# Gates in the middle of the attention, output tiles at its last units, one small load on GpSimd's queue and two column sums in two rounded parts

## The chip, the cores and the metric

The kernel runs on one core of a Trainium2 chip. A time is that of one execution on the device, in microseconds (us), and the median of several runs is compared. The core has five engines with queues of their own, which meet only at semaphores: TensorE (PE, matrix products and transposes; PEld is its weight load), VectorE (DVE), ScalarE (ACT), GpSimd (POOL) and SyncE (SP, which here only issues transfers). GpSimd can issue transfers too. Each engine works through its queue strictly in order.

## The reference

One layer of an encoder for 512 positions of width 1024, in float32, with two groups of heads side by side:

```python
h = rmsnorm(x, norm_mix); proj = h @ w_in          # c_q 768 | c_kv 256 | k_pe 32 | u_h 3 x 512
q = (rmsnorm(c_q) @ w_uq)  ; kv = rmsnorm(c_kv) @ w_ukv      # 8 heads, 64 + 32 wide keys, 64 wide values
q, k = rope(rmsnorm(q)), rope(rmsnorm(k))
y_attn = softmax(q k^T / sqrt(96)) v
x0, x1, vh = split(dwconv3(u_h))
y_hyena = x0 * (long_conv(x1 * vh, filters) + bias)          # the "gate" is this product with x0
y_mix = concat(rmsnorm(y_attn), rmsnorm(y_hyena)); x = x + y_mix @ w_out
g, u = split(dwconv3(rmsnorm(x) @ w_up)); x = x + (silu(g) * u) @ w_down
x = x + sigmoid(x @ w_ple_gate) * rmsnorm(p @ w_ple)
```

The long convolution is computed by products with cosine and sine tables. Each rmsnorm needs, for every position, the sum of squares over the features; features lie on the partitions, so that sum is a product with a matrix of ones.

## The kernel before, in words

Data lies transposed, 128 features on the partitions and 512 positions along a row. To keep float32 accuracy with the faster float32r products, each operand is split into a rounded high part (written by ACT) and the remainder (written by DVE), and each product takes three matmuls: high times high, high times low, low times high. `wload` brings a 128x1024 block of weights through SP's queue (`wr`), rounds it on ACT (`wh`), and makes the remainder on DVE, or for half of some blocks by ACT and an adding transfer of GpSimd's queue (`wl`).

The program goes through these stages: the input projection (from the first matmul at 6.3 us to 147 us, with the filters and the forward transforms of the convolution between), the keys and queries and the inverse transforms (to 196 us), the attention (scores from 196.4 to 262.0 us, its last products to 271 us), the output projection, the wide up projection with its short convolutions (to about 554 us), the down projection (to 680 us), and the gate of the embedding with the stores.

The attention is 32 units, a unit being one head for 128 of the query positions. For unit n PE makes the scores (three matmuls into `ax`), DVE takes their row maximum (`TENSOR_REDUCE st`), ACT takes the exponential (`pr`), DVE or GpSimd divides by the sum, PE transposes `pr` with the identity, ACT and DVE split the transposed block (`pth`, `ptl`), and PE multiplies it with the values (eight matmuls of 256 columns per unit pair half). The loop that emits this (`for n in range(NU + LAG + 2)`, line 1381 of before) puts two other kinds of work between the units:

- `gate(c)`, line 1227, for the four feature blocks c: four transposes on PE, three products on DVE, and for the norm a square on ACT and an add. Behind it the gated block is split (ACT and DVE) into the operands `yh`. Block 0 is emitted ahead of the loop, the others at the units named in `GN`.
- `hyena_out(m)`, line 1322, for the eight output tiles: twelve matmuls of `w_out` with `yh`, a product with the norm's factor `Rh` on DVE, a load of the block of x and an add on GpSimd. Three of the tiles are emitted at the units named in `FILLS`, five behind the loop. `Rh` is made at unit `NRH`.

Behind the loop `rms_bcast(Ra, acc5, ...)` makes the factor of the attention's norm: the ones product, then Ln and Exp with one correction step on ACT and DVE, then the products and splits of `ys` into `ya`, which the second half of the output projection reads. Four of the hyena tiles (`RFILL`) stand on PE between the ones product and the first matmul that reads `ya`.

`rms_bcast` (line 612) is called for six factors. Its ones product is in plain float32; in the trace it is two matmul records.

The order of instructions is not the order of the code. A planner (`Plan`) records all operations, gives each a due time from PE's recorded order, and then lays them out engine by engine with a cost for each kind of operation, taking at each step the earliest due of those that could start. The constants at the head (`D_...`, the delays with which side tasks are started, `GN`, `FILLS`, `NRH`, the order `UQ` of the query tiles, `TAIL`, and the table `ENG`, which says which engine does a given operation) and the allowance `MARGIN` between engines set the result.

Of the kernel before, what the change touches and what calls it, by code (L numbers as in the profile page):

```python
# [19 lines left out]
P = 128  # L20
T = 512
# [2 lines left out]
T_UQ = 3.9  # L24
T_K = 1.3
D_SIN = 2.0
D_FILT = 13.0
D_TR = 2.0
D_HALF = 7.0
D_RMS = 30.5  # L30
D_LAT = 0.0
D_UU = 13.0
D_UT = 0.5
D_MUL = 3.0
D_SPR = 3.5
D_SQ = 2.0
NTMP = 10
D_LR = 12.0
D_KC = 6.0
D_RC = 4.0  # L40
W0N = 512
W0B = 2
W1A = 3
W1B = 4
KLAG = 2.0
NRH = 15
D_FT = 8.0
TAIL = 'R E0 E1 O P V0 S0 S1 V1 S2 G0 V2 S3 V3'
ENG = {'pr0': 'G', 'a53': 'V', 'a64': 'V', 'sp3': 'V', 'pr2': 'G', 'sp7': 'G', 'qa2': 'V', 'm5': 'V', 'a51': 'G', 'ah1': 'G', 'hl0': 'V', 'fwo': 'G', 'ah3': 'G', 'qa5': 'V', 'hl2': 'G', 'qa3': 'V', 'm6': 'V', 'm7': 'G', 'm2': 'V', 'qa1': 'V', 'sp5': 'G', 'xt': 'G', 'Uc': 'G', 'sp4': 'G', 'w01': 'V', 'w11': 'V', 'a61': 'G', 'pr3': 'G', 'a67': 'G', 'a63': 'V', 'u4': 'G', 'a65': 'G', 'w10': 'G', 'u3': 'G', 'sp0': 'G', 'eos': 'V', 'vx': 'V', 'vl': 'V', 'vh': 'A', 'va': 'A', 'vf': 'V', 've': 'A', 'vc': 'A', 'sx': 'A', 'sl': 'A', 'sh': 'A', 'sa': 'V', 'sf': 'V', 'se': 'A', 'sc': 'A', 'qa4': 'G', 'sp6': 'V', 'm4': 'V', 'rot2': 'G', 'cv5': 'V', 'm1': 'G', 'a62': 'V', 'rot1': 'G', 'ah0': 'V'}
ATT = {'pr', 'a', 'ah', 'hl', 'xt'}  # L50
PRI = {'rows': 500, 'val': 20, 'kt': 60, 'rms': -120, 'cols': 400, 'H': 0, 'gate': 150, 'uT': -120, 'io': -20, 'sq': 20, 'turn': 0, 'so': -300, 'fold': -120, 't8': 0, 'gsq': -50, 'ie': 400}
QACT = 0
UQ = [5, 0, 4, 1, 2, 3]
D_KS = 2.0
D_KR = 7.0
D_TAIL = 14.5
RFILL = 4
RPRI = 0
LAG = 3
NPR = 4  # L60
FILLS = (16, 24, 32)
GN = [4, 6, 5, 11]
CPRI = 50
EPS = 1e-6
MARGIN = 0.05
AIM = 0.0
STRETCH = {'V': 1.05, 'S': 1.03, 'G': 1.05, 'PE': 1.0, 'SP': 1.0}
NH = 8
# [390 lines left out]
def tile_encoder_block(  # L459
# [19 lines left out]
    const = plan.pool("const", 1)
# [13 lines left out]
    def atile(dt=F32R):  # L493
        return apool.tile([P, T], dt, tag="a", name="a")
# [88 lines left out]
    gm = const.tile([P, 8], F32, tag="gm", name="gm")  # L583
    par = const.tile([P, NPAR], F32, tag="par", name="par")

    def pcol(name, i=0, p0=0, p1=P):
        return par[p0:p1, POFF[name] + i : POFF[name] + i + 1]

    ident = const.tile([P, P], F32, tag="ident", name="ident")
    ones = const.tile([P, P], F32, tag="ones", name="ones")  # L590
    G.memset(ones, 1.0)

    eps = const.tile([P, 1], F32, tag="eps", name="eps")
# [17 lines left out]

    def rms_bcast(out, ssq, n, tmp, key):
        ps = ax_ps()
        PE.matmul(ps, ones, ssq, start=True, stop=True)
        with pri("rms"):
            rsqrt(out, tmp(), tmp(), ps, n, key)

# [26 lines left out]
    def tmp(dt=F32):  # L644
        return ft.tile([P, T], dt, tag="t", name="t", bufs=NTMP)
# [21 lines left out]
    for k in range(8):  # L667
        t = xpool.tile([P, T], F32, tag="x", name="x")
        SP.dma_start(t, xT[k // 2][:, (k % 2) * T : (k % 2 + 1) * T])
        xraw.append(t)  # L670
        if k == 0:
            SP.dma_start(gm, g_mix)
            first = load_part(0, w0, 0, W0N)
        for at_k, m, w, a, b in ((W0B, 0, w0, W0N, 1024), (W1A, 1, w1, 0, T), (W1B, 1, w1, T, 1024)):
            if k == at_k:
                halves.setdefault(k, []).append((f"w{m}{int(a > 0)}", *load_part(m, w, a, b)))
# [4 lines left out]
    for k in range(8):  # L681
        h, l = atile(), atile()
# [9 lines left out]
    x0 = [gp.tile([P, T], F32, tag=f"x0{c}", name=f"x0{c}") for c in range(4)]  # L692
# [528 lines left out]
    yh = []  # L1221
# [5 lines left out]
    def gate(c):  # L1227
        ps = mm_ps()
        for b in range(4):
            PE.transpose(ps[:, b * P : (b + 1) * P], yt[b][:, c * P : (c + 1) * P], ident)  # L1230
        pb = ps.rearrange("p (a b) -> p a b", a=4)
        with pri("gate"):
            V.tensor_tensor(even_blocks(x0[c]), even_blocks(x0[c]), pb[:, 0:2, :], op=ALU.mult)
            V.tensor_tensor(odd_up(x0[c]), odd_up(x0[c]), pb[:, 2, :], op=ALU.mult)
            V.tensor_tensor(odd_down(x0[c]), odd_down(x0[c]), pb[:, 3, :], op=ALU.mult)
        with pri("gsq"):
            if c == 0:
                S.activation(acch, x0[c], AF.Square)
# [4 lines left out]
        with pri("so"):
            h, l = atile(), atile()
            split(h, l, x0[c], pcol("g_oh", c))
            yh.append((h, l))
# [75 lines left out]
    def hyena_out(m):  # L1322
        ps = out_mm(m, 1, yh)
        xt = xpool.tile([P, T], F32, tag="x", name="x")
        SP.dma_start(xt, xT[m // 2][:, (m % 2) * T : (m % 2 + 1) * T])
        t = tmp1()
        V.tensor_tensor(t, ps, Rh, op=ALU.mult)
        e("xt", "G").tensor_tensor(xt, xt, t, op=ALU.add)
        xm.append(xt)

    def turn(n):
# [48 lines left out]
    for n in range(NU + LAG + 2):  # L1380
        if n < NU:
            if n % 4 == 0 and 1 < n // 4 + 1 < NH:
                prep(n // 4 + 1, ap_ if n // 4 % 2 == 0 else hp)
            if n >= 4:
                scores(n)
        d = n - LAG
        if 0 <= d < NU:
            turn(d)
        d -= 1
        if 0 <= d < NU and d % 2 == 1:  # L1390
            weigh(d // 4, (d % 4) // 2)
# [313 lines left out]
```

## Time and profile before

| | us |
|---|---|
| runs of before | 726.92, 726.93, 728.01 (median 726.93) |
| the profiled execution's own time | 728.12 |
| its span, first to last instruction | 726.3 |
| PE busy | 713.0 (98%) |
| DVE busy | 504.5 (69%) |
| ACT busy | 377.9 (52%) |
| POOL busy | 178.9 (25%) |

The page gives busy times over the whole program; they are averages over stages with different limits. In the attention DVE and ACT are nearly full too, while in the up projection, half of the program, PE alone is full. PE's clock is granted in full in all of the span's slices. A matmul's end is modelled, so that a busy PE can still be slower than its best pace; the distance from one start to the next is the surer measure.

### The profile page before, as it was taken

How to read it: one execution, taken by the hardware profiler on the slowest of the kernel's cores; microseconds unless marked ns; L12 is line 12 of the kernel's file. 1: busy time of each engine (PE TensorE's matmuls, PEld its weight loads, DVE VectorE, ACT ScalarE, POOL GpSimd, SP SyncE). 2: the span in 40 equal slices, each digit the busy share in tenths (PEclk: the TensorE clock that was granted, in tenths of full speed). 3: DMA queues.
4: the chain of work that ended last, by engine and by line, in shares of the span. 5: the costliest groups of instructions: out<-in, count | busy, mean ns of one | idle time of the engine just before them, and what ended most of it. 6: DMA issues, size and time to landing. Idle time of an engine off the chain costs nothing.

```text
span 726.3 us, 9038 instructions
## 1 busy us (share of the span) xinstructions
PE 713.0 (98%) x3246; PEld 578.6 (80%) x3246; DVE 504.5 (69%) x766; ACT 377.9 (52%) x588; POOL 178.9 (25%) x158
## 2 busy tenths in 40 slices
PE   6999999999999999999999999999999999999997
PEld 4778888877677887888888888888888888888886
DVE  6689998999899978858667667667665223332383
ACT  7576554488799965636344344344343212236431
POOL 1211010111067753313322322322322000004000
PEclk9999999999999999999999999999999999999999
DMA  8488563545553223523332332332332332432331
GB/s 267 141 230 213 138 159 88 114 114 120 124 146 80 67 74 63 170 57 117 99 106 87 95 108 88 93 110 88 96 99 86 99 113 81 119 128 80 110 108 73
DMA packets 30254, 82.56 MB, mean 114 GB/s; under 512 B 3929, under 2 KB 5273, under 8 KB 30210
## 3 DMA queue, kind: packets, MB, share of 16 engines
q1 hardware_dynamic: 24818, 71.75, 32.0%
q0 software_dynamic: 5392, 10.25, 7.6%
q8 instruction: 25, 0.41, 0.2%
q14 instruction: 19, 0.16, 0.1%
HBM read 76.74 MB, written 2.10 MB: 109 GB/s over the span
## 4 chain that ended last, share of the span: by engine, by line
PE 90%; ACT 4%; DVE 3%; issue 1%; DMA 1%; POOL 1%; SPq 0%; ACTq 0%; POOLq 0%; DVEq 0%
PE mm L453 64%; PE ax L453 26%; ACT pr L453 1%; DVE st L453 1%; DMA wr<-in_w_in_dram 1%; ACT pth L453 1%; DVE ptl L453 1%; ACT a L453 0%; DVE t L453 0%; ACT t L453 0%; POOL pr L453 0%; ACT ks L453 0%; DVE a L453 0%; SPq L453 0%; DVE x L453 0%
## 5 line engine op out<-in xcount | busy, mean ns | idle before, releaser
L453 PE MATMUL mm<-a,wh 128*128 128x512 f32 (+2 forms) x928 | 310.2, 391 | 7.7 <-ACT wh L453 6.8
L453 ACT ACTIVATE wh<-wr 128x1024 fp32r<-128x1024 f32 (+2 forms) x115 | 116.6, 1016 | 188.1 <-PE mm L453 178.6
L453 PEld LDWEIGHTS mm<-a,wh 128*128 128x128 f32 (+1 forms) x928 | 173.8, 189 | 45.2 <-ACT wh L453 7.5
L453 PE MATMUL mm<-a,wl 128*128 128x512 f32 (+1 forms) x456 | 168.1, 391 | 0.0
L453 DVE TENSOR_TENSOR wl<-wr,wh 128x1024 fp32r<-128x1024 f32 (+3 forms) x115 | 119.4, 1041 | 66.9 <-ACT wh L453 66.8
L453 PE MATMUL ax<-a,wh 128*128 128x512 f32 x384 | 147.6, 389 | 0.0
L453 PEld LDWEIGHTS mm<-a,wl 128*128 128x128 f32 x456 | 86.0, 189 | 19.5 <-DVE wl L453 1.8
L453 DVE SCALAR_TENSOR_TENSOR f<-f,par,f 128x511 f32<-128x511 f32 x88 | 86.0, 981 | 2.3 <-ACT f L453 0.9
L453 PEld LDWEIGHTS ax<-a,wh 128*128 128x128 f32 x384 | 72.1, 188 | 15.0
L453 PE MATMUL mm<-g,wh 128*128 128x512 f32 x232 | 78.0, 392 | 0.0
L453 PE MATMUL ax<-a,wl 128*128 128x512 f32 x192 | 74.7, 389 | 0.0
L453 PE MATMUL mm<-h,wh 128*128 128x512 f32 x192 | 65.9, 389 | 0.0
L453 POOL TENSOR_TENSOR f<-f,f 128x512 f32<-128x512 f32 x22 | 29.8, 1357 | 141.9 <-DVE f L453 124.0
L453 PEld LDWEIGHTS mm<-g,wh 128*128 128x128 f32 x232 | 43.4, 188 | 11.4 <-issue 0.9
L453 DVE TENSOR_TENSOR f<-mm,R 128x512 f32<-128x512 f32 x22 | 15.2, 690 | 47.5 <-PE mm L453 47.5
L453 POOL TENSOR_TENSOR acc<-acc,t 128x512 f32<-128x512 f32 x13 | 18.5, 1423 | 114.6 <-ACT t L453 114.2
L453 PE MATMUL mm<-g,wl 128*128 128x512 f32 x116 | 44.0, 390 | 0.0
L453 ACT ACTIVATE f<-f 128x512 f32<-128x512 f32 x22 | 13.9, 632 | 56.1 <-DVE f L453 56.1
L453 PEld LDWEIGHTS ax<-a,wl 128*128 128x128 f32 x192 | 36.1, 188 | 7.5
L453 PEld LDWEIGHTS mm<-h,wh 128*128 128x128 f32 x192 | 36.0, 188 | 7.5
L453 ACT ACTIVATE f<-f,par 128x512 f32<-128x512 f32 x44 | 35.5, 811 | 8.3 <-DVE f L453 8.3
L453 POOL DMA_DIRECT2D wl<-in_w_in_dram x16 | 14.0, 878 | 100.7 <-ACT wl L453 68.5
(246 smaller groups left out, 1055.8 us busy)
## 6 DMA issues: line engine op xcount, KB each, us to landing
wr<-in_w_up_dram SPq DMA_DIRECT2D x44, 512.0 KB, 3.5
wr<-in_w_in_dram SPq DMA_DIRECT2D x17, 512.0 KB, 4.3
wr<-in_w_down_dram SPq DMA_DIRECT2D x16, 512.0 KB, 3.5
x<-in_xT_dram SPq DMA_DIRECT2D x16, 256.0 KB, 3.5
wl<-in_w_in_dram POOLq DMA_DIRECT2D x16, 256.0 KB, 5.5
wr<-in_w_out_dram SPq DMA_DIRECT2D x8, 512.0 KB, 4.4
wr<-in_w_gate_dram SPq DMA_DIRECT2D x8, 512.0 KB, 3.6
wr<-in_w_down_dram SPq DMA_DIRECT2D x8, 384.0 KB, 3.1
```

Of the source, the lines that this page charges most:

```text
L453: getattr(self.handles[op.eng], op.fn)(*[real(v) for v in op.args], **{k: real(v) for k, v in op.kw.items()})
```

## The change

It does five things.

1. The load of the first norm's weights (`gm`, 4 KB) goes from SP's queue, where it was the third transfer, to GpSimd's queue, where it is the first instruction of the kernel's own.
2. Gates 1 to 3 are emitted at units 12, 16 and 20, instead of 4, 5 and 6; `Rh` at unit 26, instead of 15; the three hyena tiles of the loop at 27, 32 and 34, instead of 16, 24 and 32.
3. For the factors f (ahead of the up projection) and e (the embedding's norm), the sum of squares is split into a rounded part and a remainder, and the ones product becomes two float32r matmuls.
4. In `rsqrt` the table `ENG` moves some steps between ACT and DVE: for f all to ACT, for c (the small column factors) and e two steps to DVE.
5. The planner's constants differ: delays, the order of the query tiles, the order of value and score tiles in `TAIL`, and `MARGIN` from 0.05 to 0. The branch `YFIRST` is off, and adds nothing.

```diff
-D_RMS = 30.5
+D_RMS = 34.5
...
-W1A = 3
+W1A = 4
...
-NRH = 15
+NRH = 26
...
-TAIL = 'R E0 E1 O P V0 S0 S1 V1 S2 G0 V2 S3 V3'
+TAIL = 'R E0 E1 O V0 P S0 S1 S2 G0 V1 V2 S3 V3'
...
-UQ = [5, 0, 4, 1, 2, 3]
+UQ = [0, 5, 4, 2, 3, 1]
...
-FILLS = (16, 24, 32)
-GN = [4, 6, 5, 11]
+FILLS = [27, 32, 34]
+GN = [12, 16, 20, 24]
 CPRI = 50
 EPS = 1e-6
-MARGIN = 0.05
+HALVED = 'fe'
+YFIRST = False
+MARGIN = 0
...
-    ones = const.tile([P, P], F32, tag="ones", name="ones")
+    onesr = const.tile([P, P], F32R, tag="ones", name="ones")
+    ones = f32(onesr)
...
     def rms_bcast(out, ssq, n, tmp, key):
         ps = ax_ps()
-        PE.matmul(ps, ones, ssq, start=True, stop=True)
+        if key in HALVED:
+            h, l = tmp(F32R), tmp(F32R)
+            split(h, l, ssq)
+            mms(ps, [(onesr, h), (onesr, l)])
+        else:
+            PE.matmul(ps, ones, ssq, start=True, stop=True)
...
         if k == 0:
-            SP.dma_start(gm, g_mix)
+            G.dma_start(gm, g_mix)
             first = load_part(0, w0, 0, W0N)
...
-        if n in GN and len(yh) < 4:
-            gate(len(yh))
+        if n in GN and len(gated) < 4:
+            gate(len(gated))
```

How the instructions stand is seen best in the built programs. First GpSimd's queue at the program's start, before and then with the change (`ones` and `eps` are constants that it sets; `accx` is its first addition of squares):

```order
L1700 UNCONDITIONAL_BRANCH
L453 MEMSET ones_88 128x128
L453 MEMSET eps_92 128x1
L453 ISA
L453 TENSOR_TENSOR accx_108<-accx_108,t_211 128x512
```

```order
L1721 UNCONDITIONAL_BRANCH
L455 DMA gm_88<-in_g_mix_dram 128x8
L455 MEMSET ones_94 128x128
L455 MEMSET eps_98 128x1
L455 ISA
```

The load stands ahead of the two constants. On SP all that follows the second transfer moves up by one place. On ACT the square `accx` of the first block of x stood ahead of the first split that needs `gm`, and now stands behind it.

Second, PE where the first hyena tile begins, before (`mm_2391` is the tile, `mm_2383` the product with the values, `ks,qs` scores):

```order
L453 MATMUL mm_2383<-pth_2335,g_2047 128x256
L453 MATMUL mm_2391<-a_2043,wh_1803 128x512
L453 MATMUL mm_2391<-a_2051,wh_1803 128x512
L453 MATMUL mm_2391<-a_2043,wl_1839 128x512
L453 MATMUL mm_2383<-ptl_2354,g_1965 128x256
L453 MATMUL mm_2383<-ptl_2354,g_1992 128x256
L453 MATMUL ax_2408<-ks_2124,qs_2172 128x512
L453 MATMUL mm_2383<-ptl_2354,g_2027 128x256
L453 MATMUL ax_2413<-ident_354,pr_2360 128x128 x4
```

These begin between the scores of units 13 and 14. With the change (`mm_2726` is the tile, `ax_2776` the ones product for `Rh`):

```order
L455 MATMUL mm_2726<-a_2546,wh_1785 128x512
L455 MATMUL mm_2726<-a_2389,wl_1802 128x512
L455 MATMUL mm_2726<-a_2634,wh_1785 128x512
L455 MATMUL mm_2726<-a_2716,wh_1785 128x512
L455 MATMUL mm_2726<-a_2634,wl_1802 128x512
L455 MATMUL ax_2776<-x_2039,ones_94 128x512
L455 MATMUL mm_2719<-pth_2740,g_1965 128x256
L455 MATMUL ax_2783<-ks_2571,qs_2581 128x512
L455 MATMUL mm_2719<-pth_2740,g_2024 128x256
```

The tile now begins between the scores of units 25 and 26. Counted on PE between the scores of unit 0 and those of unit 31, 26 matmuls of hyena tiles stood there before, 14 stand there now; in the last six units, 26 to 31, it was 7 and is 14, and the ones product of `Rh` stands there now. The transposes of gates 1 to 3 stood between the scores of units 4 and 8, and stand now at units 11, 15 and 19 to 20.

Third, PE where the first matmul that reads `ya` stands (`mm_3121` before and `mm_3122` with the change; `mm_3073`, `mm_3095`, `mm_3078` and `mm_3098` are hyena tiles). Before:

```order
L453 MATMUL mm_3095<-a_2190,wl_2848 128x512
L453 MATMUL mm_3073<-a_2442,wl_2848 128x512
L453 MATMUL mm_3121<-a_3108,wh_3040 128x512
L453 MATMUL mm_3095<-a_2410,wh_2801 128x512
L453 MATMUL mm_3095<-a_2428,wh_2801 128x512
L453 MATMUL mm_3121<-a_3116,wh_3040 128x512
```

With the change:

```order
L455 MATMUL mm_3098<-a_2389,wl_2983 128x512
L455 MATMUL mm_3078<-a_2747,wl_2983 128x512
L455 MATMUL mm_3122<-a_3095,wh_3042 128x512
L455 MATMUL mm_3098<-a_2634,wh_2972 128x512
L455 MATMUL mm_3122<-a_3106,wh_3042 128x512
L455 MATMUL mm_3098<-a_2716,wh_2972 128x512
```

Before, 26 rows stand between the ones product of `Ra` (`ax_3066`, row 1172 of PE) and the row that reads the first part of `ya`, and 29 up to the one that reads its remainder `a_3116`; now 33 and 35 (the ones product is row 1167).

More of the change, by code (lines that the diff above doesn't have):

```diff
@@ L26 @@
 D_SIN = 2.0
-D_FILT = 13.0
+D_FILT = 13.5
 D_TR = 2.0
 D_HALF = 7.0
-D_RMS = 30.5
+D_RMS = 34.5
 D_LAT = 0.0
@@ L33 @@
 D_UT = 0.5
-D_MUL = 3.0
-D_SPR = 3.5
-D_SQ = 2.0
+D_MUL = 3.5
+D_SPR = 7.5
+D_SQ = 8.0
 NTMP = 10
-D_LR = 12.0
+D_LR = 11.0
 D_KC = 6.0
-D_RC = 4.0
+D_RC = 4.5
 W0N = 512
 W0B = 2
-W1A = 3
+W1A = 4
 W1B = 4
 KLAG = 2.0
-NRH = 15
+NRH = 26
 D_FT = 8.0
-TAIL = 'R E0 E1 O P V0 S0 S1 V1 S2 G0 V2 S3 V3'
-ENG = {'pr0': 'G', 'a53': 'V', 'a64': 'V', 'sp3': 'V', 'pr2': 'G', 'sp7': 'G', 'qa2': 'V', 'm5': 'V', 'a51': 'G', 'ah1': 'G', 'hl0': 'V', 'fwo': 'G', 'ah3': 'G', 'qa5': 'V', 'hl2': 'G', 'qa3': 'V', 'm6': 'V', 'm7': 'G', 'm2': 'V', 'qa1': 'V', 'sp5': 'G', 'xt': 'G', 'Uc': 'G', 'sp4': 'G', 'w01': 'V', 'w11': 'V', 'a61': 'G', 'pr3': 'G', 'a67': 'G', 'a63': 'V', 'u4': 'G', 'a65': 'G', 'w10': 'G', 'u3': 'G', 'sp0': 'G', 'eos': 'V', 'vx': 'V', 'vl': 'V', 'vh': 'A', 'va': 'A', 'vf': 'V', 've': 'A', 'vc': 'A', 'sx': 'A', 'sl': 'A', 'sh': 'A', 'sa': 'V', 'sf': 'V', 'se': 'A', 'sc': 'A', 'qa4': 'G', 'sp6': 'V', 'm4': 'V', 'rot2': 'G', 'cv5': 'V', 'm1': 'G', 'a62': 'V', 'rot1': 'G', 'ah0': 'V'}
+TAIL = 'R E0 E1 O V0 P S0 S1 S2 G0 V1 V2 S3 V3'
+ENG = {'pr0': 'G', 'a53': 'V', 'a64': 'V', 'sp3': 'V', 'pr2': 'G', 'sp7': 'G', 'qa2': 'V', 'm5': 'V', 'a51': 'G', 'ah1': 'G', 'hl0': 'V', 'fwo': 'G', 'ah3': 'G', 'qa5': 'V', 'hl2': 'G', 'qa3': 'V', 'm6': 'V', 'm7': 'G', 'm2': 'V', 'qa1': 'V', 'sp5': 'G', 'xt': 'G', 'Uc': 'G', 'sp4': 'G', 'w01': 'V', 'w11': 'V', 'a61': 'G', 'pr3': 'G', 'a67': 'G', 'a63': 'V', 'u4': 'G', 'a65': 'G', 'w10': 'G', 'u3': 'G', 'sp0': 'G', 'eos': 'V', 'vx': 'V', 'vl': 'V', 'vh': 'A', 'va': 'A', 'vf': 'A', 've': 'A', 'vc': 'V', 'sx': 'A', 'sl': 'A', 'sh': 'A', 'sa': 'V', 'sf': 'A', 'se': 'V', 'sc': 'V', 'qa4': 'G', 'sp6': 'V', 'm4': 'V', 'rot2': 'G', 'cv5': 'V', 'm1': 'G', 'a62': 'V', 'rot1': 'G', 'ah0': 'V'}
 ATT = {'pr', 'a', 'ah', 'hl', 'xt'}
@@ L52 @@
 QACT = 0
-UQ = [5, 0, 4, 1, 2, 3]
+UQ = [0, 5, 4, 2, 3, 1]
 D_KS = 2.0
-D_KR = 7.0
-D_TAIL = 14.5
+D_KR = 13.0
+D_TAIL = 12.0
 RFILL = 4
@@ L1242, in gate, with split_gated @@
                 e("ah%d" % c, "G").tensor_tensor(acch, acch, sq, op=ALU.add)
[L1243 to L1246, printed above, removed]
+        gated.append(c)
+        if not YFIRST:
+            split_gated(c)
+    gated = []
+    def split_gated(c):
+        h, l = atile(), atile()
+        split(h, l, x0[c], pcol("g_oh", c))
+        yh.append((h, l))
     pend = []
@@ L1296, in tile_encoder_block, with tmp1 @@
     at = plan.pool("at", 1, reuse_waits="tile")
-    def tmp1():
-        return at.tile([P, T], F32, tag="t", name="t", bufs=3)
+    def tmp1(dt=F32):
+        return at.tile([P, T], dt, tag="t", name="t", bufs=3)
     spare[0] = tmp1
@@ L1325, in hyena_out @@
         SP.dma_start(xt, xT[m // 2][:, (m % 2) * T : (m % 2 + 1) * T])
-        t = tmp1()
-        V.tensor_tensor(t, ps, Rh, op=ALU.mult)
-        e("xt", "G").tensor_tensor(xt, xt, t, op=ALU.add)
+        if YFIRST:
+            V.tensor_tensor(xt, xt, ps, op=ALU.add)
+        else:
+            t = tmp1()
+            V.tensor_tensor(t, ps, Rh, op=ALU.mult)
+            e("xt", "G").tensor_tensor(xt, xt, t, op=ALU.add)
         xm.append(xt)
@@ L1393, in tile_encoder_block @@
                 finish(d // 4)
-        if n in GN and len(yh) < 4:
-            gate(len(yh))
+        if n in GN and len(gated) < 4:
+            gate(len(gated))
         if n == NRH:
             rms_bcast(Rh, acch, 512, tmp1, "h")
+            if YFIRST:
+                for c in range(4):
+                    V.tensor_tensor(x0[c], x0[c], Rh, op=ALU.mult)
+                    split_gated(c)
         if n in FILLS and fill < 8:
@@ L1444, in tf, with tt4 @@
         return fp.tile([P, T], F32, tag="f", name="f", bufs=8)
-    def tt4():
-        return fp.tile([P, T], F32, tag="t", name="t", bufs=2)
+    def tt4(dt=F32):
+        return fp.tile([P, T], dt, tag="t", name="t", bufs=2)
     hid = []
```

## Prediction

> **What bounds the kernel now.** I read the page's busy times first, then the waits of PE, then a table of stretches (PE, PEld, DVE, ACT and POOL busy in us, with instructions in brackets; then clock, share of the DMA engines, GB/s).
>
> ```profile
> PE 713.0 (98%) x3246; PEld 578.6 (80%) x3246; DVE 504.5 (69%) x766; ACT 377.9 (52%) x588; POOL 178.9 (25%) x158
> ```
>
> ```profile
> PE mm L453 <- ACT wh L453: 6.8, 2, 6.3
> PE mm L453 <- DVE a L453: 0.9, 1, 0.9
> PE ax L453 <- DVE st L453: 0.7, 1, 0.7
> ```
>
> ```profile
> 0.00:20.00 20.00, 13.21 (x44) 10.08 (x45) 13.10 (x20) 13.38 (x22) 3.06 (x7) 1.00 0.83 266
> 180.00:205.00 25.00, 25.00 (x117) 17.16 (x115) 21.29 (x52) 19.49 (x45) 2.95 (x4) 1.00 0.62 158
> 205.00:265.00 60.00, 58.30 (x356) 48.00 (x355) 57.01 (x141) 58.68 (x126) 46.57 (x50) 1.00 0.30 77
> 265.00:285.00 20.00, 19.13 (x95) 15.53 (x94) 13.07 (x20) 10.23 (x16) 7.08 (x7) 1.00 0.32 79
> 320.00:684.00 364.00, 364.00 (x1608) 301.30 (x1607) 206.84 (x222) 145.10 (x185) 82.79 (x51) 1.00 0.32 99
> 684.00:726.30 42.30, 38.34 (x190) 32.12 (x188) 23.48 (x33) 15.02 (x20) 0.00 (x0) 1.00 0.29 98
> ```
>
> PE sets the time: 713.0 of 726.3 us, and from 320 to 684 us it is never idle. So only two things can move the end: less work on PE, or less waiting by PE, and PE is idle for only 13.3 us in all. These lie at the start (6.8), in the attention (60.00 - 58.30 = 1.7), behind it (0.87), and behind the last matmul (42.30 - 38.34 = 4.0), where the change touches nothing. In the attention ACT (58.68 of 60) and DVE (57.01) are as full as PE; from 265 to 285 they are half empty.
>
> The unit of account is PE's pace in a full stretch, a row of the chain of waits (start, us, what):
>
> ```profile
> 554.72 96.33 PE mm L453 x425
> ```
>
> 96.33 / 425 = 0.227 us per matmul of 512 columns.
>
> **The two column sums in parts.** Rows around the ones products f and e (start, us, engine, operation; in square brackets the idle time before):
>
> ```profile
> 317.38 1.02 PE L453 MATMUL ax<-acc,ones 128*128 128x512 f32 x2
> 318.44 0.69 DVE L453 TENSOR_SCALAR t<-ax 128x512 f32<-128x512 f32 x1 [6.31 <-PE ax L453]
> 318.71 0.40 PE L453 MATMUL mm<-a,wl 128*128 128x512 f32 x1
> 319.17 0.63 ACT L453 ACTIVATE R<-t 128x512 f32<-128x512 f32 x1 [7.55 <-DVE t L453]
> ```
>
> ```profile
> 685.35 1.02 PE L453 MATMUL ax<-acc,ones 128*128 128x512 f32 x2
> 685.81 0.80 PE L453 MATMUL mm<-a,wl 128*128 128x512 f32 x1
> 686.01 1.22 DVE L453 TENSOR_TENSOR wl<-wr,wh 128x1024 fp32r<-128x1024 f32 x1 [3.21 <-ACT wh L453]
> 686.45 1.09 PE L453 MATMUL mm<-a,wh 128*128 128x512 f32 x4
> ```
>
> For e, from the ones product to the second matmul behind it: 686.45 - 685.35 = 1.10 us for it and one matmul, so 1.10 - 0.23 = 0.87. For f, 318.71 - 317.38 = 1.33 for it and two matmuls, 0.88. Two float32r matmuls are 0.45. Each saves 0.42, together **-0.8** (bounds: -0.9, and -0.4 if one comes late enough to cost its gain). The added split, one ACT and one DVE instruction of 0.63 and 0.69 as in these rows, is costed at nothing: ahead of f both engines stand idle for 6 to 7 us, ahead of e DVE for 3. Without that cover the first up tiles get their factor 1.3 us later, and PE still has products for six other PSUM buffers before it needs that one. The steps of `rsqrt` moved between ACT and DVE lie in the same idle time.
>
> **The first norm's weights.** Rows of the start, then the transfers (KB each, us to landing):
>
> ```profile
> 0.74 0.20 POOL L453 MEMSET ones<- 128x128 f32 x1 [0.29 <-POOLq L1693]
> 1.65 0.43 SPq L453 DMA_DIRECT2D gm<-in_g_mix_dram  x1
> 2.60 0.43 SPq L453 DMA_DIRECT2D wr<-in_w_in_dram  x1
> 5.01 0.72 ACT L453 ACTIVATE a<-x,gm 128x512 fp32r<-128x512 f32 x1 [0.92 <-DMA gm<-in_g_mix_dram]
> 6.30 1.22 PE L453 MATMUL mm<-a,wh 128*128 128x512 f32 x2 [6.30 <-ACT wh L453]
> 8.20 0.63 ACT L453 ACTIVATE wh<-wr 128x512 fp32r<-128x512 f32 x1 [0.81 <-DMA wr<-in_w_in_dram]
> 8.88 1.22 PE L453 MATMUL mm<-a,wh 128*128 128x512 f32 x2 [0.48 <-ACT wh L453]
> ```
>
> ```profile
> wl<-in_w_out_dram POOLq DMA_DIRECT2D x8, 256.0 KB, 4.0
> gm<-in_g_mix_dram SPq DMA_DIRECT2D x1, 4.0 KB, 3.3
> ```
>
> Issued on GpSimd's queue at 0.74, `gm` would land between 0.74 + 3.3 = 4.0 and 0.74 + 4.0 = 4.7, instead of 5.0. But ACT now does its square of 0.63 behind the first split, so the first matmul, 0.72 + 0.63 + 0.61 after `gm`, comes between 6.0 and 6.7 instead of at 6.30. What counts is the fifth, at 8.88: it waits for the second block of weights, issued at 2.60, which moves up by the 0.47 us that `gm` took on SP. DMA engines are busy for 0.83 of that stretch, so the landing moves by something between 0 and 0.47. I take **-0.3**, and -0.5 to +0.4 as its bounds.
>
> Two rules of the Trainium skill speak against this term. In "DMA: Bandwidth & Descriptors" (Issuing engine by pattern, and Specifications) transfers issued by SyncE are called generally faster, with a first byte at about 0.6 us against about 1 for GpSimd's; the rows agree in direction, 3.3 against 4.0, at unlike sizes. In "TensorE: Matmul & The Clock Gate" (What's actually happening) the slow clock at the start ends with a free-running window of about 3.4 us, not after so many matmuls; a start 0.3 us earlier would then gain half of that, and the sum below be 0.15 higher. The first matmuls here take twice the pace (1.22 us for two with the wait between), but no row tells which of the two ends it.
>
> **The exchange in the attention.** Rows, first of the third score matmul of units 0, 25 and 31, then of groups (count | busy, mean ns):
>
> ```profile
> 197.35 0.63 PE L453 MATMUL ax<-ks,qs 96*128 96x512 f32 x2
> 249.44 0.39 PE L453 MATMUL ax<-ks,qs 96*128 96x512 f32 x1
> 261.96 0.40 PE L453 MATMUL ax<-ks,qs 96*128 96x512 f32 x1
> ```
>
> ```profile
> L453 ACT ACTIVATE wh<-wr 128x1024 fp32r<-128x1024 f32 x6 | 6.4, 1066 | 1.5 <-PE mm L453 1.5
> L453 ACT ACTIVATE wl<-wr 128x512 fp32r<-128x512 f32 x6 | 3.8, 632 | 0.0
> L453 DVE TENSOR_TENSOR t<-mm,R 128x512 f32<-128x512 f32 x8 | 5.4, 682 | 0.3 <-PE mm L453 0.3
> L453 DVE TENSOR_TENSOR ptl<-ax,pth 128x512 fp32r<-128x512 f32 x32 | 21.8, 684 | 1.4 <-ACT pth L453 1.1
> ```
>
> The gates stay within the attention, so their work does not leave it; only their place changes. What leaves, counted in the built order between the first and the last unit's row maximum or exponential: on ACT one weight block (1.07 + 0.63 = 1.7 us), on DVE two products with `Rh`, one `ptl` and one step of `Rh` (4 x 0.68 = 2.7). On PE 12 matmuls of hyena tiles leave, 12 x 0.227 = 2.7. If ACT sets the pace of the units, the 64.6 us from the first to the last scores shrink by 1.7, if DVE, by 2.7. I take 2.0, nearer to ACT, which is the fuller one. The 12 matmuls are then done behind the last scores, where PE alone is full, at +2.7. Net **+0.7** (bounds 0 and +2.7: nothing shrinks). The exchange hands work to the engine that has no room, and that is why I don't expect much from the largest part of the change.
>
> **Behind the attention.**
>
> ```profile
> 275.41 1.02 PE L453 MATMUL ax<-acc,ones 128*128 128x512 f32 x2
> 281.73 1.58 POOL L453 TENSOR_TENSOR x<-x,t 128x512 f32<-128x512 f32 x1
> 281.91 1.96 DVE L453 SCALAR_TENSOR_TENSOR a<-yp,par,a 128x512 fp32r<-128x512 f32 x1
> 283.92 0.50 PE L453 MATMUL mm<-a,wh 128*128 128x512 f32 x1 [0.87 <-DVE a L453]
> 284.39 0.74 DVE L453 SCALAR_TENSOR_TENSOR a<-yp,par,a 128x512 fp32r<-128x512 f32 x1
> ```
>
> PE runs out of hyena matmuls and waits 0.87 us for the remainder of `ya`, which took 1.96 instead of 0.74 while GpSimd added a tile. In the new order 35 matmuls stand between the ones product and that reader, not 29: 6 x 0.227 = 1.4 us more cover, more than the wait. **-0.9** (bounds -1.0 and 0).
>
> The planner's constants, the query order and the new order of gates shift many other rows. I cost them at nothing: between 180 and 205 us PE is busy for 25.00 of 25, and work that is only reordered in front of a full PE doesn't change its sum. If a row now waits there, it costs what it waits; I keep 0.5 either way.
>
> Sum: -0.8 - 0.3 + 0.7 - 0.9 = **-1.3 us**. The profiled execution took 728.12, its span 726.3; with the change 726.8 and 725.0. The median of the runs, 726.93, is 1.2 below that execution, and becomes **725.6**.
>
> **The rivals.**
>
> *The gates were the trouble* (20 in 100). All 1.7 us of PE's idle time in the attention lie there while gates and tiles crowd ACT and DVE; spread out, they go too, and the units keep an even pace. Then 725.6 - 1.7 = 723.9. For it: the wait for `st` (0.7) in the first units. Against it: ACT has 1.3 us free in 60, so there is little to even out.
>
> *The late tiles stand in front of the last scores* (13 in 100), the slower side. In units 26 to 31, 12.5 us long (261.96 - 249.44), 14 hyena matmuls stand instead of 7, and the ones product of `Rh`: 7 x 0.227 + 0.87 = 2.5 us more in front of scores on which ACT waits; while in units 4 to 25 PE has nothing to fill in, and a unit's own chain from scores to exponential to transposes keeps the old pace, so that nothing shrinks. Exchange 2.7 + 2.5 = 5.2; sum -0.8 - 0.3 + 5.2 - 0.9 = +3.2, 730.1. It decides from an exchange of +3.5 on. For it: PE's order is strict. Against it: PE had 52 us for 26 units whose work is less.
>
> *The moves come to nothing* (7 in 100): `gm` lands late, at +0.4, and the wait for `ya` stays since GpSimd's adds still stand in DVE's way. -0.8 + 0.4 + 0.7 = +0.3: 727.2.
>
> **How the numbers follow.** The forecast has 60 in 100, with a range of its own from 724.4 to 726.8. The measurement tells about 0.2% (1.45 us) from no change, so faster is below 725.5 and slower above 728.4. Of the forecast's 60 some 25 lie below 725.5; with the first rival faster has 45. Same has the forecast's other 35 and the third rival's 7, 42. Slower has 13. The range of 8 in 10 reaches to the first rival and some way to the slower one: 723.3 to 728.4.
>
> **What would show it.** The ones products f and e as two rows at the common pace. ACT's first split before 5.0 us, and the pair of matmuls of 8.88 at 8.4 to 8.9. The last unit's scores 1.7 to 2.7 us earlier than now relative to the first unit's. No wait of PE for `a` near 283 us. I am wrong in the exchange if that distance shrinks by 3 or more, or doesn't shrink; and if PE shows a wait between 140 and 200 us, in what I costed at nothing.

## The result, and the profile after

| | before | with the change |
|---|---|---|
| median of the runs, us | 726.92 (726.09 to 728.01, 4 runs) | 734.21 (733.52 to 735.65, 4 runs) |
| ratio, 95% interval | | 1.0095 (1.0079 to 1.0110) |
| span of the profiled execution, us | 726.3 | 732.4 |

The kernel became slower by about 1%, where 725.6 was forecast in a range up to 728.4. Of the profile after, first the page's busy times, then PE's waits, then the stretches (columns as in the prediction; the fourth and fifth row go from the exponential of unit 0 to that of unit 25, and from there to that of unit 31).

```profile
PE 714.5 (98%) x3246; PEld 578.2 (79%) x3246; DVE 510.0 (70%) x773; ACT 379.0 (52%) x585; POOL 179.9 (25%) x159
```

```profile
PE mm L455 <- ACT wh L455: 7.5, 1, 7.5
PE mm L455 <- DVE wl L455: 1.9, 1, 1.9
PE ax L455 <- ACT pr L455: 1.8, 4, 0.7
PE ax L455 <- DVE ptl L455: 1.5, 1, 1.5
PE mm L455 <- ACT t L455: 0.4, 1, 0.4
```

```profile
0.00:20.00 20.00, 12.45 (x44) 9.94 (x45) 12.90 (x20) 13.07 (x22) 3.84 (x8) 1.00 0.82 265
180.00:205.00 25.00, 25.00 (x110) 16.11 (x110) 21.27 (x52) 16.68 (x34) 1.48 (x3) 1.00 0.53 124
205.00:265.00 60.00, 56.26 (x340) 45.90 (x339) 54.81 (x141) 58.09 (x127) 43.01 (x47) 1.00 0.32 87
202.64:253.78 51.14, 47.40 (x287) 38.67 (x286) 47.00 (x125) 49.92 (x110) 37.18 (x41) 1.00 0.38 101
253.78:267.82 14.04, 14.04 (x86) 11.49 (x85) 12.83 (x31) 12.25 (x26) 7.66 (x9) 1.00 0.17 57
265.00:285.00 20.00, 20.00 (x106) 16.42 (x105) 13.88 (x25) 11.21 (x20) 10.77 (x10) 1.00 0.36 80
```

The wait for `ya` (0.9, `DVE a`) is gone, as forecast. There is a new one of 1.9 for `wl`. In the attention PE is idle for 60.00 - 56.26 = 3.7 us instead of 1.7. And from 180 to 205 us PE is again busy for 25.00 of 25. But at their usual distances the 115 instructions that begin there before come to 23.1 us, the 109 with the change to 22.6: a stretch that is full can still lose.

**Lost time at landmarks.** Busy time does not show such a loss, so I worked out another measure from the traces. For each form of PE instruction take the median distance from its start to the next start in the trace of before (0.227 us for a 128x512 float32r product). Add these up over all instructions ahead of a landmark, whatever their order, and subtract the sum from the landmark's start. What is left is what PE has lost until there.

| lost up to, us | before | after | difference |
|---|---|---|---|
| first ones product (23 us) | 10.15 | 10.26 | +0.1 |
| first scores (196 and 200 us) | 14.50 | 17.73 | +3.2 |
| last scores (262 and 265 us) | 22.93 | 28.42 | +5.5 |
| ones product of `Ra` | 23.26 | 29.05 | +5.8 |
| ones product f | 24.83 | 31.67 | +6.8 |
| last matmul | 25.26 | 31.26 | +6.0 |

So the start cost nothing, 3.1 us went ahead of the attention, 2.3 into it, 0.3 and 1.1 behind it, and f and e gave 0.8 back. The two spans differ by 6.1, as the table; the medians by 7.3. The profiled execution of before (728.12 us) took 1.2 longer than the median of its kernel, that of the change (734.29) only 0.1.

### The profile page after: what moved, and what is told of

Read it like the earlier page. It is cut to its first block, busy times and chain, and to the rows that moved or that the text cites. A ratio compares the mean times of both kernels' runs of the same rounds, so it can differ in the third digit from the quotient of the medians.

```text
span 732.4 us, 9056 instructions
## 1 busy us (share of the span) xinstructions
PE 714.5 (98%) x3246; PEld 578.2 (79%) x3246; DVE 510.0 (70%) x773; ACT 379.0 (52%) x585; POOL 179.9 (25%) x159
## 4 chain that ended last, share of the span: by engine, by line
PE 90%; DVE 4%; ACT 3%; DMA 2%; issue 1%; DVEq 0%; SPq 0%; ACTq 0%; POOLq 0%
PE mm L455 63%; PE ax L455 27%; DVE t L455 2%; DMA wr<-in_w_in_dram 1%; DVE wl L455 1%; ACT pr L455 1%; DVE g L455 1%; DMA gm<-in_g_mix_dram 1%; DVE st L455 0%; DMA wr<-in_w_out_dram 0%; ACT t L455 0%; ACT wh L455 0%; DVE ptl L455 0%; ACT pth L455 0%; DVE a L455 0%
## 5 line engine op out<-in xcount | busy, mean ns | idle before, releaser
L455 DVE TENSOR_TENSOR wl<-wr,wh 128x1024 fp32r<-128x1024 f32 (+3 forms) x115 | 122.3, 1067 | 67.3 <-ACT wh L455 67.3
```

What stands on the lines that cost most here:

```text
L455: getattr(self.handles[op.eng], op.fn)(*[real(v) for v in op.args], **{k: real(v) for k, v in op.kw.items()})
```

## The experiments

Each run's profile was read with the same table. Below are the differences from the profiled execution of before, stretch by stretch; a star marks a fall of PE's clock to one half for 3.4 us (below), which costs up to 1.7 us each; where the text leaves a fall out, it takes off these 1.7. In e10 to e12 the time of the added products counts as lost.

| run | ratio to before, 95% interval | start | to first scores | to last scores | to `Ra` | to f | f and e | sum |
|---|---|---|---|---|---|---|---|---|
| the change | 1.0095 (1.0079-1.0110) | +0.1 | +3.1 | +2.3 | +0.3 | +1.1 | -0.8 | +6.0 |
| e1 places only | 1.0057 (1.0041-1.0073) | -1.5 | +0.8 | +4.2* | +0.6 | +0.3 | 0 | +4.5 |
| e2 constants only | 1.0051 (1.0031-1.0071) | -0.3 | +4.2* | +0.5 | +0.2 | 0 | 0 | +4.7 |
| e3 no places | 1.0026 (1.0014-1.0039) | -1.5 | +3.1 | +0.1 | +0.2 | 0 | -0.8 | +1.1 |
| e4 parts and queue | 1.0011 (1.0000-1.0021) | -1.2 | +0.8 | +2.2* | 0 | 0 | -0.9 | +1.0 |
| e5 adds on DVE | 1.0053 (1.0034-1.0073) | -1.6 | +3.5 | +2.3 | +0.3 | -1.1 | -0.8 | +2.4 |
| e6 tiles only | 1.0094 (1.0064-1.0123) | -1.5 | +1.2 | +6.6* | +0.1 | +0.3 | 0 | +6.9 |
| e7 gates only | 1.0092 (1.0056-1.0127) | -0.1 | +1.3 | +5.2** | +0.1 | +2.0 | 0 | +8.4 |
| e8 old queries | 1.0081 (1.0052-1.0110) | -1.3 | +5.6** | +3.1 | +0.1 | +1.0 | -0.8 | +7.8 |
| e9 parts and adds | 0.9994 (0.9981-1.0007) | -0.2 | +0.2 | +1.0 | +0.1 | -1.1 | -0.9 | -0.9 |
| e10 with 11 products | 0.9988 (0.9973-1.0002) | -1.8 | +0.5 | +0.9 | +0.1 | -1.1 | -0.8 | -2.2 |
| e11 with 15 products | 0.9978 (0.9965-0.9990) | -1.2 | +0.2 | +0.9 | +0.1 | -1.1 | -0.8 | -1.9 |
| e12 mix | 0.9979 (0.9966-0.9992) | -1.8 | +0.5 | +0.9 | 0 | -1.1 | -0.8 | -2.3 |
| e13 delays old | 1.0095 (1.0072-1.0118) | +0.8 | +3.6 | +2.3 | +0.2 | +1.1 | -0.8 | +7.2 |
| e14 MARGIN only | 1.0051 (1.0032-1.0069) | -1.8 | +1.0 | +1.9 | +0.5 | +0.2 | +0.1 | +1.8 |

Kernels whose order ahead of the scores is that of before (e1, e4, e6, e7, e9) lose 0.2 to 1.3 more there than the one execution of before, nearly all of it at 40 to 60 us. That much differs from execution to execution; of the change's 3.1, the 2.3 behind 60 us are its own.

### The change taken apart: e1 to e4

```diff
-NRH = 15
+NRH = 26
-FILLS = (16, 24, 32)
-GN = [4, 6, 5, 11]
+FILLS = [27, 32, 34]
+GN = [12, 16, 20, 24]
```

That is e1, on the kernel before; e2 has instead the thirteen other constants of the change (D_..., W1A, TAIL, UQ, MARGIN), e3 is the change with the three lines above as before, and e4 the kernel before with `HALVED = 'fe'`, the changed `ENG` and `gm` on GpSimd's queue.

> The kernel before with only the places of gates, output tiles and Rh of the change. Ledger theory (lost time of PE at landmarks, after less before: 3.1 us up to the first scores, 2.3 between the first and the last scores, 0.3 up to Ra's ones product, 1.1 from there to f): the places make everything from the first scores to f, so this kernel is 2.3 + 0.3 + 1.1 = 3.7 us slower than before, and nothing is lost ahead of the scores. Rival (the constants and the query order do it all): this kernel is -0.2 us from before, as predicted for the exchange and the cover of Ra together (0.7 - 0.9). Rival (only the combination is slow): within 1 us of before.

> The kernel before with only the planner's constants of the change (delays, query order, TAIL, the second block's load, MARGIN 0). Ledger theory: 3.1 us slower than before, all of it lost ahead of the first scores, the attention as before within 0.5. Rival (constants do it all): 6.9 us slower, with 2 to 3 us lost in the attention. Rival (only the combination): within 1 us of before.

> The changed kernel with the places of gates, tiles and Rh as before. Ledger theory: 3.7 us faster than the change, 2.3 slower than before. Constants-do-it-all: as slow as the change, 6 above before. Only the combination: 0.7 us faster than before (the parts f and e gain 0.84, the start loses 0.1).

> The kernel before with the column sums f and e in two parts, the moved steps of rsqrt and gm on GpSimd's queue; places and constants as before. All theories: 0.7 us faster than before (-0.84 by the two ones products, +0.1 at the start). The first matmul comes 1.2 us later than before, the loss at the first ones product is 0.1. If the new splits or steps make a wait of PE of their own, it is slower than that and shows behind f or e.

The ledger theory holds, and the two rivals fall: the places alone and the constants alone are each half a per cent slower, at different places. Without its starred fall e1 loses 2.5 between the first and the last scores, and nothing of its own ahead of them; e2 loses 2.5 ahead of the scores and 0.5 in the attention. The times say the same: the record gives the mean granted clock of every execution, and those of e1 and e2 with 0.999 or 1.000 (three each) have medians of 731.3 and 730.9 us, 3.2 and 2.7 above such executions of before (728.1), where 3.7 and 3.1 were expected. Taken out of the change, the places give back what was lost behind the first scores (e3). But the loss behind `Ra`, put down to the places, is in neither of the two (0.3 and 0): the wait for `wl` needs both. In e4 f and e gain 0.85, and yet it is not faster than before (0.7 us were expected). Its profile has a fall of PE's clock in the attention, but the falls are not the reason: six of its twelve executions have a mean clock of 0.998 (median 729.4 us), and the other six, at 0.999 or 1.000, have 728.1, as before has. Without the fall its profile still loses 0.5 in the attention, and 0.8 at 40 to 60 us; what makes the 0.5 is not shown.

### What stands behind the wait for `wl`: e5

In the trace of the change, where PE waits at 296.37 (only the rows of the engines that take part):

```profile
288.11 3.57 DVE L455 SCALAR_TENSOR_TENSOR a<-yp,par,a 128x512 fp32r<-128x512 f32 x3
288.86 1.60 POOL L455 TENSOR_TENSOR x<-x,t 128x512 f32<-128x512 f32 x1
292.80 4.11 DVE L455 TENSOR_TENSOR wl<-wr,wh 128x512 fp32r<-128x512 f32 x2
292.95 2.80 POOL L455 TENSOR_TENSOR x<-x,t 128x512 f32<-128x512 f32 x2
296.37 0.50 PE L455 MATMUL mm<-a,wl 128*128 128x512 f32 x1 [1.86 <-DVE wl L455]
```

Two instructions of 0.68 took 4.11. In both traces every VectorE instruction that takes over 0.3 us more than the median of its form overlaps a GpSimd one, and it ends 0.54 to 0.56 us after the GpSimd one that held it (0.8 and 1.1 for two blocks, of 768 and 1024 columns); its operands all lie in SBUF. Products with an operand in PSUM, as `t<-mm,R` (0.68), run at their usual time beside the same adds. The 1.96 instead of 0.74 that the prediction quoted is the same thing: 281.73 + 1.58 = 283.31, and 281.91 + 1.96 = 283.87. In the trace of e2 the same pair of `wl` begins half a microsecond ahead of the adds, and holds them instead (3.15 for two, 1.29 each in the records of an undisturbed one):

```profile
292.81 1.28 DVE L455 TENSOR_TENSOR wl<-wr,wh 128x512 fp32r<-128x512 f32 x2
293.36 3.15 POOL L455 TENSOR_TENSOR x<-x,t 128x512 f32<-128x512 f32 x2
```

The Trainium skill has this in "SBUF — State Buffer" (SBUF: two separate sides): VectorE with two SBUF inputs and GpSimd share a pair of ports under an exclusive lock, and who starts first holds it for its whole instruction. The traces agree in the lock, with two additions. Two GpSimd adds in a row held `wl` for both, 3.5 us. And the start in the record does not tell who holds: the held `wl` begins at 292.80, 0.15 us ahead of the add that holds it (292.95), while in e2 a `wl` that begins 0.55 us ahead is the one that holds.

> The changed kernel with one letter of the table ENG changed: the adds of the hyena output tiles to x (x<-x,t) are done by VectorE, not GpSimd; PE's instructions and their order are the same as in the change. Lock theory: the wait of PE for wl at 294 us in the change (1.9) is there because a VectorE instruction with two operands in SBUF ends 0.55 us after a GpSimd add that overlaps it; without the adds on GpSimd no wl takes over 0.8 us there, the wait goes, and PE loses 1.8 to 2.0 us less between Ra's ones product and f than in the change. Rival (the blocks of weights come too late by transfer or rounding): the wait for wl stays, within 0.4. Rival (VectorE becomes the bound by the eight adds of 0.68): the wait moves to another VectorE product, and nothing is gained.

```diff
-ENG = {..., 'xt': 'G', ...}
+ENG = {..., 'xt': 'V', ...}
```

```profile
289.11 0.68 DVE L455 TENSOR_TENSOR wl<-wr,wh 128x512 fp32r<-128x512 f32 x1
290.31 0.68 DVE L455 TENSOR_TENSOR wl<-wr,wh 128x512 fp32r<-128x512 f32 x1
290.90 1.28 DVE L455 TENSOR_TENSOR x<-x,t 128x512 f32<-128x512 f32 x2
```

With PE's order unchanged (and no GpSimd add of the tiles left) the wait is gone, and PE loses 2.2 us less from `Ra` to f than in the change (-1.1 against +1.1). The adds cost VectorE 0.64 each and nobody waits. The lock is the cause; both rivals fall.

### Gates or tiles: e6 and e7

e6 has only the lines NRH and FILLS of e1's diff, e7 only GN. In e7 the first tile and `Rh` come before all gates are done: the tile leaves out the product with block 3, and the sum for `Rh` the squares of two blocks.

> The kernel before with only the late output tiles (27, 32, 34) and Rh at unit 26; gates as before. Theory (PE has nothing to fill in with in the middle units, the units keep their own pace, and the 12 matmuls are done behind): PE loses 2 to 2.7 us more than before between the first and the last scores (without a drop of PE's clock, which is told apart by the granted clock). Rival (the gates crowd the middle): within 0.5 of before.

> The kernel before with only the gates 1 to 3 at units 12, 16 and 20; tiles and Rh as before (a tile waits for its gate, so tiles of the loop may be emitted behind). Theory of late tiles: PE loses between the first and the last scores as much as before, within 0.5, without a drop of the clock. Rival (gates in the middle crowd VectorE and ScalarE there): 2 to 2.7 more.

Without the falls of the clock e6 loses 4.9 and e7 1.8, both together (e1) 2.5. So the tiles weigh more, but my theory that the gates cost nothing finds no support, and the two don't add up. Neither number is what the theory gave (2 to 2.7 and at most 0.5), e7 does not compute the same as the others, and why the tiles alone cost twice what both together cost stays open. What the change itself does in the attention is read from its two stretches above, beside those of before:

```profile
199.02:251.94 52.92, 51.33 (x305) 41.91 (x304) 50.05 (x129) 52.00 (x113) 38.72 (x42) 1.00 0.35 100
251.94:263.96 12.02, 11.91 (x77) 10.01 (x77) 11.71 (x29) 10.95 (x24) 8.89 (x11) 1.00 0.38 89
```

Units 0 to 25 take 51.14 us instead of 52.92; with fewer tiles to do PE is busy for 47.40 of it, idle for 3.7 instead of 1.6. The units have become 1.8 us shorter, while PE's work there fell by 51.33 - 47.40 = 3.9: the rest turned into waits for `pr` (1.8) and `ptl` (1.5), the chain of a unit itself. In units 25 to 31 PE is full in both, and the tiles and the ones product of `Rh` that now stand there lengthen them by 2.0 (14.04 - 12.02). From the first to the last exponential nothing has shrunk (65.2 and 64.9), and from the third score matmul of unit 0 to that of unit 31 only 0.3 (64.6 before, 64.3 now); and the 12 matmuls are still to be done behind it.

### What a full PE loses ahead of the scores: e8, e13, e14

Four 8x8 transposes in the trace of before, and the same four with the change, which stand apart there (PE):

```profile
172.22 0.61 PE L453 MATMUL mm<-g,wl 128*128 128x512 f32 x2
172.76 0.41 PE L453 MATMUL ax<-ident,t 8*128 8x8 f32 x4
173.10 0.72 PE L453 MATMUL mm<-g,wh 128*128 128x512 f32 x2
```

```profile
172.42 0.61 PE L455 MATMUL mm<-g,wh 128*128 128x512 f32 x2
172.97 0.22 PE L455 MATMUL ax<-ident,t 8*128 8x8 f32 x1
173.12 0.50 PE L455 MATMUL mm<-g,wh 128*128 128x512 f32 x1
173.55 0.22 PE L455 MATMUL ax<-ident,t 8*128 8x8 f32 x1
173.71 0.50 PE L455 MATMUL mm<-g,wh 128*128 128x512 f32 x1
174.14 0.22 PE L455 MATMUL ax<-ident,t 8*128 8x8 f32 x1
174.29 0.73 PE L455 MATMUL mm<-g,wl 128*128 128x512 f32 x2
174.96 0.22 PE L455 MATMUL ax<-ident,t 8*128 8x8 f32 x1
175.11 0.50 PE L455 MATMUL mm<-g,wh 128*128 128x512 f32 x1
```

From one transpose to the next with a single product between them it is 0.58 us (173.55 - 172.97), of which the product is 0.227 and the transpose some 0.06: a change into such work and out of it costs some 0.3, whether one transpose stands there or four. PE is "busy" throughout. In a run of products the trace has each load of weights (PEld) begin 0.2 us ahead of its product (174.40 and 174.63); here it begins with the product (173.119 and 173.120). That the loads are the reason is likely, but no run varies them. Transposes, full-float32 products and the products of 40 rows (`selT`) form 20 stretches ahead of the scores before, and 25 with the change. From 155 us to the first scores the change loses 1.7 more than before, 1.4 of it at the edges of such stretches or within them.

> The changed kernel with the order of the query tiles and three delays (D_SQ, D_RMS, D_KR) as before. Theory (what the constants lose ahead of the first scores is mostly the price of switching PE between full-float32 products or transposes and float32r products, 0.3 us for each stretch of them; 25 stretches stand there with the change, 21 in this kernel, 20 before): PE loses 1.2 us less between 60 us and the first scores than the change (2.3 more than before there). Rival (waits for operands): the same loss of 2.3.

```diff
-D_RMS = 34.5
+D_RMS = 30.5
-D_SQ = 8.0
+D_SQ = 2.0
-UQ = [0, 5, 4, 2, 3, 1]
+UQ = [5, 0, 4, 1, 2, 3]
-D_KR = 13.0
+D_KR = 7.0
```

```profile
174.66 0.41 PE L455 MATMUL ax<-ident,t 8*128 8x8 f32 x4
```

The transposes stand together again. Less the fall of the clock at 195.4 us (up to 1.7), PE loses 1.15 more than before between 65 us and the scores, the change 2.3: 1.2 less, as the theory had it. Measured as a whole e8 is no faster than the change (735.29 us); four of its five executions have a mean clock of 0.998 or less, the profiled one with two falls, and the fifth, at 1.000, took 731.90.

Of the change's 2.3 that leaves a loss of 0.6 at 150 to 153 us, where ScalarE and VectorE now round a block of weights in front of the operand (`t`) for which PE is shown to wait 0.4 (rows of the change):

```profile
149.51 0.85 ACT L455 ACTIVATE wh<-wr 128x768 fp32r<-128x768 f32 x1 [1.30 <-PE mm L455]
150.77 0.55 DVE L455 TENSOR_TENSOR wl<-wr,wh 128x384 fp32r<-128x384 f32 x1
153.12 0.62 ACT L455 ACTIVATE t<-accy 128x512 fp32r<-128x512 f32 x1
153.27 0.73 PE L455 MATMUL mm<-g,wh 128*128 128x512 f32 x2 [0.40 <-ACT t L455]
```

e13 and e14 ask which constants make it.

> The changed kernel with the delays of the filter, the transforms and the moving of weights (D_FILT, D_MUL, D_SPR, D_LR, D_RC, W1A) as before; MARGIN 0 and query order as in the change. If these delays make the wait at 152 us (0.6, a block of weights rounded ahead of the operand that PE waits for) and the loss at 40 to 60 us (0.5 to 0.7 more than before), both go: 1.1 to 1.3 less lost up to the first scores than in the change. If MARGIN makes them: both stay.

> The kernel before with MARGIN 0 in place of 0.05 and nothing else. If MARGIN makes the wait at 152 us and the loss at 40 to 60 us, they show here: 1.1 to 1.3 more lost up to the first scores than before. If the delays make them: as before up to the first scores within 0.3 (beside the phase of the clock at the start).

In e13 the loss stays (0.6), in e14 it is there (0.7): it comes from MARGIN. The loss at 40 to 60 us follows neither (1.3 in e13, 0.3 in e14) and belongs to what differs between executions. MARGIN alone makes the kernel half a per cent slower, and most of that lies in the attention (1.9), where PE waits for `st` (1.2), `pth` (0.9) and `t` (0.7). Yet all constants together (e2) lose only 0.5 there: how they act on each other was not taken further apart.

### A version that is faster than both: e9 to e12

e9 is the kernel before with f and e in two parts, the changed `ENG`, and the tiles' adds on VectorE. e10 and e11 add, as PE's first work, products whose results are not used; e12 is e11 with the adds of the three tiles in the loop back on GpSimd.

```diff
+    warm = ax_ps()
+    for _ in range(15):
+        PE.matmul(warm[:, 0:P], ones, ones, start=True, stop=True)
+        plan.ops[-1].dur = 0.0
```

> The kernel before with the column sums f and e in two parts and the moved steps of rsqrt, and with the hyena tiles' adds to x on VectorE in place of GpSimd; places, constants and gm as before. Lock theory: no VectorE product behind Ra takes over 0.8 us, the wait of PE for ya (0.9 at 284 us) goes, and f and e gain 0.84: 1.9 us faster than before where the clock of PE takes the same course. Rival (VectorE has no room in the attention): the three adds of the loop, 0.68 each, cost up to 2.0 between the first and the last scores, and the sum is 0.

> The kernel of the run with parts and adds, and 11 full-float32 products of the matrix of ones with itself (128 columns, results not used) as PE's first work, while it has nothing to do; PE's order behind them is the same. Clock theory (PE's clock goes to full at the end of a window of 3.41 us that PE filled, windows that run on from before the kernel): the products take 0.43 each at half clock, from 1.1 to some 5.8 us, the clock is full between 4.5 and 7.9 us and not between 10.2 and 13.2 as in all traces so far, and PE loses 1.5 to 2.5 us less at its first ones product; up to 0.8 of it is given back at 40 to 50 us, where the filter's chain on ScalarE and VectorE is fixed by transfers. Rival (the start is set by transfers): the clock is full earlier, but PE waits for weights and x instead, and nothing is gained.

> The same with 15 products, which end at 6 to 7.5 us. Clock theory: as with 11; where the clock is not full by 6.5 us the first product of the input projection comes up to 1 us later than with 11, but no window between lets the clock fall back. Rival (start set by transfers): as slow as without them or up to 1 us slower.

> The kernel before with f and e in two parts, the 15 early products of ones, and the adds of the five tiles behind the loop on VectorE, those of the loop on GpSimd. Theory: the adds in the loop cost the run with all adds on VectorE 1.0 between the first and the last scores, and come back here, while the wait for ya stays away: 1.0 us faster than the run with 15 products, some 2.6 below before. Rival (the planner spends it elsewhere): as the run with 15 products, 0.2% below before.

e9 shows both repairs where they were expected (-1.1 and -0.9), but loses 1.0 in the attention. It is no different from before by its interval; half of its twelve executions have a mean clock of 0.997 or less, of before 1 in 29 at the same time. The adds are not what costs that 1.0: in e12, with the loop's adds back on GpSimd, 0.9 stays, and e12 is not the 1.0 us better that I had expected. What makes it stays open.

The early products bring the full clock as early as the clock theory said: it is recorded from 5.47, 4.94 and 4.32 us on in e10, e11 and e12, in the other traces from 10.2 to 14.0. In e11:

```profile
1.00 5.47 PE L455 MATMUL ax<-ones 128*128 128x128 f32 x30 [1.00 <-POOL eps L455]
6.51 0.76 PE L455 MATMUL mm<-a,wh 128*128 128x512 f32 x2
8.95 0.74 PE L455 MATMUL mm<-a,wh 128*128 128x512 f32 x2 [0.84 <-ACT wh L455]
```

The first pair of real products takes 0.76, not 1.22. PE then waits for weights (0.84). The 1.5 to 2.5 expected are not shown: at the first ones product e10 to e12 have lost 1.2 to 1.8 less than the one execution of before, but so have e1, e3 to e6, e8 and e14 without such products (1.2 to 1.8). e11 (726.54 us) and e12 (726.15) are 0.2% faster than before (728.01 and 727.87 beside them); how much of that the early products give is not told apart, since the interval of e9, which has none, overlaps theirs.

## Why the prediction was wrong

By its steps, with the difference of lost time as the measure:

| step | forecast | measured |
|---|---|---|
| f and e in two parts | -0.8 | -0.84 |
| `gm` on GpSimd's queue | -0.3 | +0.1, not told apart from the clock's phase |
| exchange in the attention | +0.7 | +2.6 |
| cover behind `Ra` | -0.9 | +1.1 (the wait of 0.9 gone, one of 1.9 come) |
| constants and query order | 0 (0.5 either way) | +2.3, and 0.8 that varies |

- **The column sums were right**: two rows of 0.39 at the common pace (in the trace at 323.99 and 324.45 for f), and nothing waits for the added split.
- **"I cost them at nothing ... work that is only reordered in front of a full PE doesn't change its sum" was the step that failed most.** It isn't so: five more stretches of transposes and other slow forms, 0.3 us each, are 1.5 us with no wait in the profile. The row I had leaned on, 25.00 of 25 busy, reads the same after the change, and hides 1.9 us of loss before and 2.4 after. Another 0.6 is made by MARGIN, of which the profile shows 0.4 as a wait.
- **The exchange was right in its first half.** I gave the units a shrinking of 2.0, and the first 25 shrank by 1.8. I left out that seven of the remaining matmuls and `Rh`'s ones product move into the last six units, where PE is full: +2.0. That is what the slower rival described, with 2.5 for it; its other half, that the middle units keep their pace, did not come. With the 12 matmuls behind the scores the sum is 2.7 - 1.8 + 2.0 = 2.9 by the units, 2.6 by the landmarks. The chance of 13 in 100 was too small for a rival whose place and price I had worked out.
- **The cover behind `Ra` came as forecast, and was lost ten microseconds later.** I had taken the 1.96 as one delay to be covered. It was a lock between two engines, and the adds that hold it still stand there. Moved by the new order, they now hold a `wl`, which has no cover. The third rival had named those adds and put them in the way of `ya`.
- **The start** did not gain. GpSimd's issue begins at 1.27 us, not 0.74, and takes 0.75; over the traces of all runs `gm` lands between 4.9 and 6.8 us by SP (ten traces) and between 4.8 and 6.2 by GpSimd (six), so the row of 3.3 us I built on was one of a spread. The first matmul moved from 6.30 to 7.55 and cost only 0.1: the clock went to full at 13.22 us before and at 13.01 with the change. (The page's row of the clock, and the 1.00 of the stretch from 0 to 20 us, read full from the start; but the trace's record of the clock begins at 13.22, and PE works on 9 instructions in the 3.41 us ahead of that, on 16 in the 3.41 us behind.) The rule I had weighed from the Trainium skill, "TensorE: Matmul & The Clock Gate" (What's actually happening), that the slow clock ends by time and not by work, is the one that these two times bear out.

Of the signs of being wrong that I had named, the wait between 140 and 200 us came (0.4), and the distance between the first and the last unit's scores shrank by 0.3 where 1.7 to 2.7 had been forecast, next to the "doesn't shrink" that was to refute the exchange.

## What to carry to other kernels

Where an engine is full, reordering still costs or saves: in this kernel it paid to count how often PE changes between kinds of work, not only how long it is busy. The stall that came from two engines excluding each other was not cured by cover at the place where it showed; it moved to what the held engine did next. Taking the holder away did cure it (one letter, 2.2 us). And when work is moved out of a stretch, ask for each of the places it leaves and enters whether the bound engine is full there: here leaving a place with waits gave back 1.8 of 3.9 us of work, and entering a full one cost 2.0 of 2.5.

## What the runs showed of the hardware

**The clock of PE falls in the middle of the kernel.** In six of the profiled executions PE's granted clock drops to one half for 3.413 us (in e7 for twice that, in e8 at two places). The rows of e4 (columns as before, the clock is the third from the end):

```profile
202.27:205.69 3.42, 3.42 (x22) 2.82 (x20) 3.12 (x12) 2.67 (x9) 0.90 (x2) 1.00 0.77 282
205.69:209.10 3.41, 1.87 (x10) 1.02 (x9) 3.37 (x8) 3.41 (x8) 2.30 (x3) 1.00 0.03 5
209.10:212.52 3.42, 3.42 (x14) 3.23 (x15) 2.09 (x7) 3.42 (x8) 3.42 (x4) 0.50 0.42 94
212.52:215.93 3.41, 3.41 (x26) 2.91 (x25) 3.01 (x9) 2.38 (x6) 2.62 (x4) 1.00 0.60 136
```

PE was busy for 1.87 of 3.41 us, with no wait of over 0.62, and then did 14 instructions in a window where it does 22 to 26 otherwise. The windows run on without regard to the kernel: from the moment at which the clock first went to full to the later fall it is 197.97 us in e4 (209.10 - 11.13) and in e1 (208.14 - 10.17), 58 times 3.413; 180.90 in e2, 53 times; 225.28 in e6, 66 times. In before the thin stretch behind 206 us lies across the end of a window (207.78), and there is no fall. What it takes for a fall is not shown: ahead of five of the seven falls PE was busy for 1.6 to 2.2 us of the window, but ahead of those in e2 (193.64) and e8 (195.42) for all of it (20 and 19 instructions, transposes and other slow forms among them); and in the trace of the change a window with 1.60 us of work (292.90 to 296.32) was followed by none. Executions of one kernel differ by it: those of e4 whose mean clock shows a fall took 1.3 us longer than the others. The Trainium skill, "TensorE: Matmul & The Clock Gate" (What's actually happening), states a free-running window of that length, and these rows agree; it has the clock fall after an idle window, while here one that was half busy was enough.

**The same windows set the start.** The first ones product comes at 23.11 us where the clock is full from 13.22, at 22.94 from 12.36, at 21.63 from 10.17 and at 21.31 from 10.34, whatever the first matmul's time was (6.30, 7.58, 6.23 and 6.32). Over the thirteen traces without early products it comes between 21.31 and 23.91 us: 2.6 us by chance, as much as most of the effects in this study. With the early products it is 21.29 to 21.89, the early end of that range.
